# Wider rearranging DMAs for raw keys and values, key copies by DMA, and first queries' lower halves on VectorE, in a planned attention stage

## The chip, the cores and the metric

The kernel runs on one core of a Trainium2 chip. The metric is the time on the device in microseconds: the median of several executions. One execution was also taken by the hardware profiler; all rows below are of that one. Engines are named as the profile has them: PE is TensorE (matmuls; PEld its weight loads), DVE is VectorE, ACT is ScalarE, POOL is GpSimd, SP is SyncE, which here only issues DMAs.

## The reference

A decoder of two layers over 512 tokens of width 1024. Layer 0 is a gated short convolution and a squared-ReLU MLP. Then one shared key and value side is projected; layer 1 is sparse attention over it (16 heads in 4 groups of 64 channels) and another MLP. What matters here, cut down:

```python
def compress_blocks(t, pe, w1, w2):                    # t: (B,S,G,dh), blocks of 32, stride 16
    chunks = t.reshape(B, S // 16, 16, G, dh)
    blocks = jnp.concatenate([chunks[:, :-1], chunks[:, 1:]], axis=2) + pe[None, None, :, None, :]
    flat = jnp.moveaxis(blocks, 2, 3).reshape(B, 31, G, 32 * dh)
    return jax.nn.silu(flat @ w1) @ w2

kv = (rms_norm(x, kv_norm) @ w_kv).reshape(B, S, 6, N_KV_GROUPS, HEAD_DIM)
k_raw, v_raw, k_sel, v_sel, k_win, v_win = ...          # the six parts
k_cmp = compress_blocks(k_raw, cmp_pe_k, phi_k_w1, phi_k_w2)
v_cmp = compress_blocks(v_raw, cmp_pe_v, phi_v_w1, phi_v_w2)
# per query block: softmax attention over k_cmp, over selected blocks (all 8 of them, top_n = 16 > 8),
# and over the window of 512; the three are weighted by gates and summed; then w_o, then the MLP
```

With 512 tokens there are 8 selection blocks, fewer than the 16 that may be selected, and the window covers all tokens, so two of the three branches are full causal attention with their own keys and values.

## The kernel before, in words

All matrix products are made from 16-bit floats with each operand split in a high and a low half (`hi` is the rounded value, `lo` the rest), so one product is three matmuls. Activations lie transposed, channels on the 128 partitions and 512 tokens along the row; a `new_split` gives a pair of tiles, [128, 8, 512] each, for the halves.

Weights stream from memory in pieces. SyncE issues the load of a piece into one of three buffers `wst`; ScalarE converts it to `whi`, VectorE subtracts to get `wlo`, and the buffer is free for the piece three further on. Pieces are loaded and converted in the order in which they are used.

From 500 to 800 us runs the attention stage. Its instructions are not issued as the code meets them: they are held (`Plan.hold`), and `Plan.issue` writes out one order for each engine by simulating them. It knows each task's cost (`Plan.cost`, from constants per engine and the number of elements), how long a result takes to reach another engine, and when a DMA lands (`Plan.land`: 2050 ns and bytes over 325 per ns). A task becomes ready when those it depends on end; an engine takes the ready task with the smallest key, that is, the earliest in the code. Which tasks depend on each other `Plan.touch` finds from the box (partitions, first to last element of the row) that each operand spans. The order is fixed at build time; at run time each engine works in order and waits only for what its operands really need.

In that stage, `keys(br)`, `values(br)`, `queries(g)`, `gates`, `raw(which)` and `phi(which)` are background work, cut in units that a list of names, costs and due times (`AGENDA`) spreads between the attention items. The items (`Full`: a group, a block of 128 queries, a branch) compute scores (`st0`), exponentials, transposes, and products with values; `Cmp` items do the compressed branch. `keys(0)` and `queries(0)` come first; no item can begin without them.

- `keys(br)`: the product with the weights gives two PSUM banks `po`; each is scaled to `t` and holds two groups, 64 channels each on partitions 0–63 and 64–127. The score matmuls use all 128 rows: the query tile holds the query's high half on one set of 64 partitions and its low half on the other, and so the keys must stand on both. `KD[r, br, 0, g]` and `KD[r, br, 1, g]` are the high and low half on the group's own partitions `r`, `KD[o, ...]` the same on the other 64, `o`. Before, ScalarE and VectorE compute both copies.
- `queries(g)`: `q[r, h]` on ScalarE is the high half, `q[o, h]` on GpSimd the low half on the other partitions.
- `raw(which)` makes the keys (0) or values (1) that `phi(which)` compresses. Tokens are reordered so that the 16 places in a chunk come first (`r`, 16) and the 32 chunks follow (`b`, 32); `hl` holds the halves. `phi` multiplies for each of 16 pairs of places, so partitions 0–63 must hold a row and 64–127 the same row 32 columns on. This shift across partitions is done by DMAs from SyncE, into `big` for the keys and into the pair named `xs` (`xsh` and `xsl` in the profile) for the values.
- `phi` reads 31 columns from `at = 64 * (cc % 8) + cc // 8` on, for `cc` from 0 to 15.

Of the kernel before, what the change touches and what calls it, by code (L numbers as in the profile page):

```python
# [10 lines left out]
F32 = mybir.dt.float32  # L11
F16 = mybir.dt.float16
AF = mybir.ActivationFunctionType
OP = mybir.AluOpType
PSUM = bass.MemoryType.PSUM
DRAM = bass.MemoryType.DRAM


S, D, F, H, G, DH = 512, 1024, 4096, 16, 4, 64
# [26 lines left out]
class Plan:  # L46
# [83 lines left out]
    def cost(self, name, op, args, kwargs, out, ins):  # L130
        n = max(self.count(a) for a in out + ins)
        if name == "PE":
            n = self.count(out[0])
            if op == "transpose":
                return max(84.0, n / 128 * 109)
            if ins[0].dtype == F32:
                return 223.0 if n == 1 else n * 1.7
            return max(25.3, n * 0.4213)
        if "dma" in op:
            return 370.0  # L140
        if op == "memset":
            return 50 + 0.8 * n
        slope = self.SLOPE[name]
        if op == "tensor_copy" and ins[0].dtype == F16:
            slope *= 0.35
        return self.BASE[name] + slope * n + (189 if kwargs.get("accum_out") is not None else 0) + (
            20 if op == "tensor_tensor_reduce" else 0)

    def land(self, t, at):
# [74 lines left out]
class Held:  # L224
    ins = None
# [20 lines left out]
def body(ctx, tc, x, rel_bias, norm_mix, norm_mlp, mlp_w1, mlp_w2, a_w_in, a_conv_w, a_w_out,  # L246
# [4 lines left out]
    PE, ACT, DVE, POOL, SPQ = (plan.engine(e) for e in ("PE", "ACT", "DVE", "POOL", "SP"))  # L251
# [3 lines left out]
    work = ctx.enter_context(pool("work"))  # L255
# [206 lines left out]
    xt4 = wk[0].tile([128, 4, D], F32, name="xt")  # L462
    xt = [xt4[:, t] for t in range(4)]
# [28 lines left out]
    gain = {"mix0": 0, "mix1": 8, "mlp0": 16, "mlp1": 24, "kv": 32}  # L492

    def new_split(p, name, bufs=1):
        return tuple(p.tile([128, 8, S], F16, name=name + e, bufs=bufs) for e in "hl")

    def split_gain(dst, c, src, gname):

        g = vec[:, gain[gname] + c:gain[gname] + c + 1]
        hi = ACT.activation(dst[0][:, c], src, AF.Copy, scale=g)  # L500
        DVE.scalar_tensor_tensor(dst[1][:, c], src, g, dst[0][:, c], op0=OP.mult, op1=OP.subtract)
        return hi
# [67 lines left out]
    def ftile(name, bufs=2, n=S):  # L570
        return wk[0].tile([128, n], F32, name=name, bufs=bufs)

    def split_to(hi, lo, src, scale=1.0):
        ACT.activation(hi, src, AF.Copy, scale=scale)
        if scale == 1.0:
            DVE.tensor_tensor(lo, src, hi, op=OP.subtract)
        else:
            DVE.scalar_tensor_tensor(lo, src, scale, hi, op0=OP.mult, op1=OP.subtract)


    xs = new_split(wk[0], "x0")

    def x_chunk(c):
# [16 lines left out]


    ys = new_split(wk[0], "y")
    for p in range(4):
        pc, pu, pb = [], [], []
# [41 lines left out]
        for dst in (pc, pu, pb):  # L646
# [7 lines left out]
            for m in range(2):  # L654
                ch = 2 * p + m
                if dst is pc:
                    if m == 0:
                        tmps = []
                    t = ftile("cv_t", 2)
                    DVE.scalar_tensor_tensor(t, pc[m], 1.0 / (SY * SY), rb2, op0=OP.mult, op1=OP.mult)  # L660
                    tmps.append(t)
                elif dst is pu:
# [6 lines left out]
                    o = ftile("cv_o", 2)  # L669
# [13 lines left out]
    xs = new_split(work, "xs")  # L683
# [114 lines left out]
    def first_half(hp, xs, ss):  # L798
        rh = tuple(hp.tile([128, 8, 7, 256], F16, name=n) for n in ("rh", "rl"))
        rb = mlp_up(xs, ss, rh, 0, None)  # L800
        mlp_down(rh, None)
        mlp_up(xs, ss, rh, 1, rb)
        return rh
# [18 lines left out]
    with pool("attn") as ap_:  # L822
# [8 lines left out]
        KD = ap.tile([128, 2, 2, G, S], F16, name="KD")  # L831
# [30 lines left out]
        def rows_after_first():  # L862
            nonlocal rbk, rbq, rtok
            r = ss.r
            pr = broadcast_rows(r)
            rbk = row_tile(pr, SK / (SW * SX))
            rbq = row_tile(pr, SQ / 8.0 / (SW * SX))
            rtok = ap.tile([128, 2, 4], F32, name="rtok")
            DVE.tensor_scalar(rtok[:, 0], r, SV / (SW * SX), None, op0=OP.mult)
            DVE.tensor_scalar(rtok[:, 1], r, 0.5 / (SW * SX), None, op0=OP.mult)  # L870

        def scaled(ps, rb):
            t = ftile("at_s", 3)
            DVE.tensor_tensor(t, ps, rb, op=OP.mult)
            return t
# [6 lines left out]
        def gated_pair(xs, mid=None):  # L882

            po = [abank(), abank()]
            for half in range(2):
                w = next_piece()
                cv = ahead_fine()
                for c in range(4):
                    if mid and (half, c) == (1, 1):
                        mid()  # L890
                    for m in range(2):
                        k = 4 * half + c
                        mm3(po[m], [u[:, c, m * 128:(m + 1) * 128] for u in w], [u[:, k] for u in xs],
                            k == 0, k == 7)
                        next(cv, None)
                        yield 0.65
                drain(cv)
            return po
# [6 lines left out]
        def keys(br):  # L905
            po = yield from gated_pair(xkv, ss.rstd if rbk is None else None)
            if rbk is None:
                rows_after_first()
            for m in range(2):
                t = scaled(po[m], rbk)  # L910
                for s in range(2):
                    g, r = 2 * m + s, slice(64 * s, 64 * s + 64)
                    o = slice(64 - 64 * s, 128 - 64 * s)
                    ACT.activation(KD[r, br, 0, g], t[r], AF.Copy)
                    ACT.activation(KD[o, br, 0, g], t[r], AF.Copy)
                    DVE.tensor_tensor(KD[r, br, 1, g], t[r], KD[r, br, 0, g], op=OP.subtract)
                    DVE.tensor_tensor(KD[o, br, 1, g], t[r], KD[r, br, 0, g], op=OP.subtract)
                yield
            if br == 0:
                for c in range(8):  # L920
                    split_gain(xq, c, X[:, c], "mix1")
# [42 lines left out]
        def queries(g):  # L964
            po = yield from gated_pair(xq)
            q = ap.tile([128, 4, S], F16, name="Q", bufs=4)
            for m in range(2):
                t = scaled(po[m], rbq)
                for s in range(2):
                    h, r = 2 * m + s, slice(64 * s, 64 * s + 64)  # L970
                    o = slice(64 - 64 * s, 128 - 64 * s)
                    ACT.activation(q[r, h], t[r], AF.Copy)
                    POOL.tensor_tensor(q[o, h], t[r], q[r, h], op=OP.subtract)
                yield
            Qs[g] = q


        def raw(which):
            po = yield from gated_pair(xkv)
            if which == 0:  # L980
                both = ap.tile([128, 2, 8, S], F16, name="big", bufs=1)
                kr = [both[:, hl] for hl in range(2)]
            else:
                kr = new_split(work, "xs")
            for u in kr:
                DVE.memset(u[:, 4], 0.0)
                DVE.memset(u[64:128, 0:4, S - 1:S], 0.0)
            for half in range(2):
                at = slice(half, S, 64)
                split_to(kr[0][:, 4, at], kr[1][:, 4, at], pet[:, which, 8 * half:8 * half + 8], SK)  # L990
            both = ap.tile([128, 4, S], F16, name="kr_hl", bufs=1)
            for m in range(2):
                t = ftile("at_s", 3)
                by_stride = lambda a: a.rearrange("p (b r) -> p r b", r=16)
                DVE.tensor_tensor(t.rearrange("p (r b) -> p r b", r=16), by_stride(po[m]), by_stride(rbk),
                                  op=OP.mult)
                hl = both[:, 2 * m:2 * m + 2]
                split_to(hl[:, 0], hl[:, 1], t)
                for s in range(2):
                    g, r = 2 * m + s, slice(64 * s, 64 * s + 64)  # L1000
                    for k, u in enumerate(kr):
                        SPQ.dma_start(u[0:64, g, :], hl[r, k])
                        SPQ.dma_start(u[64:128, g, 0:S - 32], hl[r, k, 32:S])
                        SPQ.dma_start(u[64:128, g, S - 32:S - 1], hl[r, k, 1:32])
                yield
            KRs[which] = kr

# [376 lines left out]
        for i in range(len(items) + 6):  # L1384
# [8 lines left out]
            while credit > 0.0:  # L1393
                u = next(bg, "end")
# [15 lines left out]
    xs = xm  # L1410
# [3 lines left out]
    with pool("hidden_b") as hp:  # L1414
        wk[0] = hp
        rh = first_half(hp, xs, ss)
        xt = [work.tile([128, 2, D], F32, name=n) for n in ("xsh", "xsl")]
        xt = [xt[t // 2][:, t % 2] for t in range(4)]
        fng = [work.tile([128, S], F32, name="rb", bufs=3) for _ in range(2)]
        for half in range(2):  # L1420
            POOL.dma_start(fng[half], bass.AP(tensor=final_norm.tensor, offset=final_norm.offset + half * S,
                                                   ap=[[0, 128], [1, S]]))
# [137 lines left out]
```

## Time and profile before

| | |
|---|---|
| median of 3 runs | 1129.56 us (1128.71 to 1130.78) |
| profiled execution, own time | 1129.92 us |
| its span | 1128.2 us |
| mean granted TensorE clock | 0.993 of full speed |
| TensorE busy | 1095.0 us (97%) |
| VectorE busy | 875.1 us (78%) |
| ScalarE busy | 572.2 us (51%) |
| GpSimd busy | 56.2 us (5%) |

The span runs from the first to the last instruction of the profiled execution; its own time is a little longer. Busy times of engines overlap. A row of instructions reads: start and length in us (or a count with least, median and greatest length in ns), the engine, the line of the kernel, the operation, what it writes `<-` what it reads, the shapes, and in brackets how long the engine was idle before it and what ended that. Everything in the planned stage carries line 206, where the plan issues it, so rows there are told apart by their tiles. `SPq` is SyncE issuing DMAs: the length of such a row is the issue, not the transfer.

### The profile page before, as it was taken

The numbers are of one execution on the slowest core, as the hardware profiler recorded it, in microseconds if no ns is written. First come the engines' busy times: TensorE is split into PE (matmuls) and PEld (weight loads), VectorE is DVE, ScalarE is ACT, GpSimd is POOL, SyncE is SP. The second block draws the span as 40 slices with busy tenths as digits, with TensorE's granted clock in tenths as the row PEclk, the third lists the DMA queues.
The fourth block names the chain that finished last, engine by engine and source line by source line (L and its number), as shares of the span: only waits on it lengthen the run. The fifth ranks groups of instructions, "written<-read, shape, count | busy, mean of one in ns | idle before, by whom it ended". The sixth has DMA issues, their size and how long they took to land.

```text
span 1128.2 us, 20034 instructions
## 1 busy us (share of the span) xinstructions
PE 1095.0 (97%) x7959; PEld 695.6 (62%) x7959; DVE 875.1 (78%) x1642; ACT 572.2 (51%) x920; POOL 56.2 (5%) x71
## 2 busy tenths in 40 slices
PE   8999999999999999999999799899999999999996
PEld 4444444447884448876666676675444788444895
DVE  4755457987988768969688689997998798865776
ACT  3532244554334435547577679765754434442352
POOL 0000000000000000002010022212000000000010
PEclk9999999999999999999999899999999999999999
DMA  6433334533343332322324351012553333330221
GB/s 209 124 105 94 112 94 150 165 115 110 102 123 116 96 91 77 93 75 84 114 76 114 98 156 55 27 33 76 165 165 100 113 113 113 112 94 1 92 78 75
DMA packets 150050, 115.76 MB, mean 103 GB/s; under 512 B 9028, under 2 KB 146980, under 8 KB 149956
## 3 DMA queue, kind: packets, MB, share of 16 engines
q1 hardware_dynamic: 147120, 108.94, 32.3%
q10 hardware_dynamic: 2548, 4.93, 1.3%
q8 instruction: 62, 1.02, 0.4%
q0 software_dynamic: 288, 0.61, 0.2%
q14 instruction: 32, 0.26, 0.1%
HBM read 110.22 MB, written 2.14 MB: 100 GB/s over the span
## 4 chain that ended last, share of the span: by engine, by line
PE 83%; DVE 9%; ACT 2%; DMA 2%; issue 2%; SPq 1%; POOL 1%; DVEq 0%; ACTq 0%; POOLq 0%
PE c L240 23%; PE b L240 21%; PE a L240 20%; PE a L206 7%; PE d L240 4%; PE c L206 3%; DVE at_s L206 3%; PE e L240 2%; PE b L206 2%; DVE at_pl L206 2%; PE d L206 1%; SPq L206 1%; DVE wlo L206 1%; DVE o_t L206 1%; DMA xt<-x_dram 1%
## 5 line engine op out<-in xcount | busy, mean ns | idle before, releaser
L240 PEld LDWEIGHTS <-whi 128*128 128x128 f16 x3328 | 325.6, 98 | 200.9 <-issue 2.7
L240 ACT ACTIVATE whi<-wst 128x1024 f16<-128x1024 f32 (+2 forms) x162 | 209.2, 1297 | 279.1 <-PE b L240 96.4
L240 DVE SCALAR_TENSOR_TENSOR wlo<-wst,whi 128x1024 f16<-128x1024 f32 (+2 forms) x162 | 245.8, 1522 | 54.6 <-ACT whi L240 54.4
L240 PEld LDWEIGHTS <-wlo 128*128 128x128 f16 x1664 | 162.8, 98 | 101.5 <-issue 0.6
L240 DVE TENSOR_TENSOR wst<-wst 128x256 f32<-128x256 f32 x256 | 94.9, 418 | 21.4 <-DMA wst<-mlp_w_dram 20.2
L240 DVE TENSOR_TENSOR rl<-ml_z,rh 128x1792 f16<-128x1792 f32 x32 | 64.7, 2023 | 44.4 <-ACT rh L240 44.4
L240 ACT ACTIVATE rh<-ml_z 128x1792 f16<-128x1792 f32 x32 | 54.3, 1697 | 66.5 <-DVE ml_z L240 66.5
L206 ACT ACTIVATE at_p<-at_s,at_m 128x128 f32<-128x128 f32 (+3 forms) x128 | 70.9, 554 | 24.0 <-DVE at_m L206 22.6
L206 PEld LDWEIGHTS <-whi 128*128 128x128 f16 x512 | 48.0, 98 | 41.5 <-issue 4.2
L240 PE MATMUL c<-xsh,whi 128*128 128x512 f16 x192 | 72.8, 379 | 0.0
L240 PE MATMUL c<-xsl,whi 128*128 128x512 f16 x192 | 72.8, 379 | 0.0
L240 PE MATMUL c<-xsh,wlo 128*128 128x512 f16 x192 | 72.8, 379 | 0.0
L240 PE MATMUL b<-xsl,whi 128*128 128x512 f16 x192 | 72.8, 379 | 0.0
L240 PE MATMUL b<-xsh,wlo 128*128 128x512 f16 x192 | 72.8, 379 | 0.0
L240 PE MATMUL b<-xsh,whi 128*128 128x512 f16 x192 | 72.7, 379 | 0.0
L240 PE MATMUL c<-rh,whi 128*128 128x256 f16 x256 | 69.8, 273 | 0.0
L240 PE MATMUL c<-rh,wlo 128*128 128x256 f16 x256 | 69.8, 273 | 0.0
L240 PE MATMUL c<-rl,whi 128*128 128x256 f16 x256 | 69.8, 273 | 0.0
L240 PE MATMUL a<-rh,whi 128*128 128x256 f16 x256 | 69.1, 273 | 0.0
L240 PE MATMUL a<-rh,wlo 128*128 128x256 f16 x256 | 69.1, 273 | 0.0
L240 PE MATMUL a<-rl,whi 128*128 128x256 f16 x256 | 67.8, 273 | 0.0
L206 DVE SCALAR_TENSOR_TENSOR at_pl<-c,at_ph 128x512 f16<-128x512 f32 (+2 forms) x96 | 59.2, 618 | 9.5 <-ACT at_ph L206 9.3
(275 smaller groups left out, 2311.4 us busy)
## 6 DMA issues: line engine op xcount, KB each, us to landing
wst<-mlp_w_dram SPq DMA_DIRECT2D x256, 256.0 KB, 3.4
wst<-a_w_in_dram SPq DMA_DIRECT2D x18, 512.0 KB, 3.6
wst<-w_kv_dram SPq DMA_DIRECT2D x12, 512.0 KB, 3.7
T<-ext_d ACTq DMA_DIRECT2D x4, 1056.0 KB, 6.9
wst<-a_w_out_dram SPq DMA_DIRECT2D x8, 512.0 KB, 3.6
wst<-b_w_qg_dram SPq DMA_DIRECT2D x8, 512.0 KB, 3.8
wst<-b_w_o_dram SPq DMA_DIRECT2D x8, 512.0 KB, 3.6
wst<-a_w_in_dram SPq DMA_DIRECT2D x8, 384.0 KB, 5.9
```

The source lines that it names most:

```text
L206: getattr(self.engines[t["e"]], t["op"])(*t["args"], **t["kw"])
L240: return real(*args, **kwargs)
```

## The change

It has five parts.

1. `raw`: the tile for both halves is one, and each DMA moves both halves of a group to one set of partitions. The columns from 480 on are no longer filled: the third, short DMA goes, the long ones are cut to 480 columns, and the memset of the last column goes. 8 DMAs per call instead of 24.
2. `keys`: the copy on the other partitions is made by one DMA per group, from the copy just computed, instead of by a ScalarE and a VectorE instruction. 4 DMAs per call.
3. `queries`: for g = 0 the low halves are computed by VectorE, for the others by GpSimd as before.
4. The plan's costs: a DMA whose source is on the chip costs 640 instead of 370; instructions over at most 64 partitions and more than 256 elements cost 110 more; `scalar_tensor_tensor` on VectorE with a one-element operand 60 more; `tensor_tensor` over rows of 16 in reordered steps has 1.75 times the slope.
5. `new_split` gives the two halves of one tile, [128, 2, 8, 512], instead of two tiles; the names that share its memory follow (`xs`).

```diff
         if "dma" in op:
-            return 370.0
+            return 370.0 if ins[0].space == DRAM else 640.0
...
-        slope = self.SLOPE[name]
+        slope, base = self.SLOPE[name], self.BASE[name]
         if op == "tensor_copy" and ins[0].dtype == F16:
             slope *= 0.35
-        return self.BASE[name] + slope * n + (189 if kwargs.get("accum_out") is not None else 0) + (
+        if out[0].ap[0][1] <= 64 and n > 256:
+            base += 110
+        elif name == "DVE" and op == "scalar_tensor_tensor" and any(self.count(a) == 1 for a in ins):
+            base += 60
+        if op == "tensor_tensor" and ins and list(ins[0].ap)[-1][0] == 16:
+            slope *= 1.75
+        return base + slope * n + (189 if kwargs.get("accum_out") is not None else 0) + (
...
     def new_split(p, name, bufs=1):
-        return tuple(p.tile([128, 8, S], F16, name=name + e, bufs=bufs) for e in "hl")
+        t = p.tile([128, 2, 8, S], F16, name=name, bufs=bufs)
+        return t[:, 0], t[:, 1]
...
                     ACT.activation(KD[r, br, 0, g], t[r], AF.Copy)
-                    ACT.activation(KD[o, br, 0, g], t[r], AF.Copy)
                     DVE.tensor_tensor(KD[r, br, 1, g], t[r], KD[r, br, 0, g], op=OP.subtract)
-                    DVE.tensor_tensor(KD[o, br, 1, g], t[r], KD[r, br, 0, g], op=OP.subtract)
+                    SPQ.dma_start(KD[o, br, :, g], KD[r, br, :, g])
...
-                    POOL.tensor_tensor(q[o, h], t[r], q[r, h], op=OP.subtract)
+                    (POOL if g else DVE).tensor_tensor(q[o, h], t[r], q[r, h], op=OP.subtract)
...
-            if which == 0:
-                both = ap.tile([128, 2, 8, S], F16, name="big", bufs=1)
-                kr = [both[:, hl] for hl in range(2)]
-            else:
-                kr = new_split(work, "xs")
-            for u in kr:
-                DVE.memset(u[:, 4], 0.0)
-                DVE.memset(u[64:128, 0:4, S - 1:S], 0.0)
+            both = (ap.tile if which == 0 else work.tile)([128, 2, 8, S], F16, name="xs" if which else "big", bufs=1)
+            kr = [both[:, hl] for hl in range(2)]
+            DVE.memset(both[:, :, 4], 0.0)
...
-            both = ap.tile([128, 4, S], F16, name="kr_hl", bufs=1)
+            whole = ap.tile([128, 4, S], F16, name="kr_hl", bufs=1)
...
-                    for k, u in enumerate(kr):
-                        SPQ.dma_start(u[0:64, g, :], hl[r, k])
-                        SPQ.dma_start(u[64:128, g, 0:S - 32], hl[r, k, 32:S])
-                        SPQ.dma_start(u[64:128, g, S - 32:S - 1], hl[r, k, 1:32])
+                    SPQ.dma_start(both[0:64, :, g, 0:S - 32], hl[r, :, 0:S - 32])
+                    SPQ.dma_start(both[64:128, :, g, 0:S - 32], hl[r, :, 32:S])
...
-        xt = [work.tile([128, 2, D], F32, name=n) for n in ("xsh", "xsl")]
-        xt = [xt[t // 2][:, t % 2] for t in range(4)]
+        xt4 = work.tile([128, 4, D], F32, name="xs")
+        xt = [xt4[:, t] for t in range(4)]
```

More of the change, by code (lines that the diff above doesn't have):

```diff
@@ L996, in raw @@
                                   op=OP.mult)
-                hl = both[:, 2 * m:2 * m + 2]
+                hl = whole[:, 2 * m:2 * m + 2]
                 split_to(hl[:, 0], hl[:, 1], t)
```

## The prediction

> **What bounds the kernel now.** I read the page's summary first, then TensorE's stretches in the attention part, then the waits and the SyncE queue there.
>
> ```profile
> span 1128.2 us, 20034 instructions
> PE 1095.0 (97%) x7959; PEld 695.6 (62%) x7959; DVE 875.1 (78%) x1642; ACT 572.2 (51%) x920; POOL 56.2 (5%) x71
> ```
>
> The stretches (us from the span's start, length, busy time of each engine, granted clock), first the whole attention part, then four pieces of it with what follows them:
>
> ```profile
> core 0: us, PE busy (x) PEld busy (x) DVE busy (x) ACT busy (x) POOL busy (x), PEclk, DMA share, GB/s
> 500.00:800.00 300.00, 280.83 (x2836) 192.60 (x2834) 253.74 (x683) 216.60 (x546) 45.28 (x50) 0.98 0.29 87
> 508.00:528.00 20.00, 17.47 (x117) 10.59 (x116) 18.88 (x32) 14.66 (x27) 6.19 (x4) 1.00 0.26 80
> 560.00:564.00 4.00, 2.71 (x16) 1.39 (x14) 3.79 (x9) 3.95 (x11) 0.00 (x0) 1.00 0.00 0
> 615.00:617.40 2.40, 0.37 (x4) 0.09 (x3) 2.03 (x10) 1.36 (x6) 0.61 (x1) 1.00 0.27 58
> 617.40:621.00 3.60, 3.60 (x31) 3.24 (x32) 1.49 (x3) 2.07 (x5) 0.00 (x0) 0.53 0.75 193
> 621.00:634.40 13.40, 13.40 (x206) 12.29 (x203) 12.67 (x35) 8.10 (x22) 1.47 (x2) 1.00 0.33 73
> 634.40:641.20 6.80, 0.17 (x3) 0.00 (x0) 0.37 (x2) 1.66 (x4) 0.00 (x0) 0.76 0.73 218
> 641.20:644.40 3.20, 3.15 (x25) 2.56 (x26) 2.18 (x7) 3.13 (x11) 0.00 (x0) 0.50 0.10 33
> ```
>
> TensorE is 97% busy over the span, but 300 − 280.83 = 19.2 us of its 33.2 us idle lie in the planned attention part. Four stretches hold 12.5 us of that: 2.5 in 508–528, 1.3 in 560–564, 2.0 in 615–617.4, 6.6 in 634.4–641.2. After the last two the granted clock is about 0.5, the 1.2 GHz level, for 3.6 and 3.2 us. In the longest, VectorE and ScalarE do almost nothing either (0.37 and 1.66 us), so its whole length is on the path. Who waited for whom there (us in total, times, longest):
>
> ```profile
> PE a L206 <- DMA big<-kr_hl: 2.0, 1, 2.0
> ```
> ```profile
> ACT whi L206 <- DMA wst<-b_w_qg_dram: 7.8, 1, 7.8
> ...
> PE c L206 <- ACT at_p L206: 6.7, 1, 6.7
> ```
> ```profile
> PE b L206 <- DVE xql L206: 1.4, 1, 1.4
> PE a L206 <- ACT GT L206: 1.3, 1, 1.3
> PE b L206 <- POOL Q L206: 1.1, 3, 0.8
> ```
>
> And SyncE's queue, with the conversions that its weight loads feed or wait for:
>
> ```profile
> 596.54 19.73 SPq L206 DMA_DIRECT2D big<-kr_hl  x24
> ...
> 617.82 3.66 SPq L206 DMA_DIRECT2D xsh<-kr_hl  x6
> ...
> 632.08 2.97 SPq L206 DMA_DIRECT2D xsl<-kr_hl  x3
> 635.14 0.53 SPq L206 DMA_DIRECT2D wst<-b_w_qg_dram  x1
> ```
> ```profile
> 639.54 1.06 ACT L206 ACTIVATE whi<-wst 128x1024 f16<-128x1024 f32 x1 [7.83 <-DMA wst<-b_w_qg_dram]
> ```
> ```profile
> 625.65 1.29 DVE L206 SCALAR_TENSOR_TENSOR wlo<-wst,whi 128x512 f16<-128x512 f32 x2
> ```
>
> The 6.7 us is a weight load in the wrong place. SyncE issues the 48 rearranging copies of raw(0) and raw(1) almost without a pause from 596.5 to 635.1, and the second load of q2's weights stands behind them all. It is issued at 635.14. ScalarE, which works in order, stopped at 631.7 (639.54 − 7.83) to convert it; the exponentials behind it (at_p) come late, and TensorE with them. The 2.0 us is phi(0), waiting for raw(0)'s last copy.
>
> **The change part by part.**
>
> ```profile
> L206 SPq DMA_DIRECT2D big<-kr_hl x24: 462/595/1762, 596.5 to 615.5; - x24
> ...
> L206 DVE TENSOR_TENSOR kr_hl<-at_s,kr_hl x4: 681/690/692, 596.5 to 621.5; 128x512 f16<-128x512 f32 x4
> ...
> DMA to landing us min/median/max: 1.8/2.7/7.8
> ```
> ```profile
> big<-kr_hl SPq DMA_DIRECT2D x8, 64.0 KB, 3.7
> ...
> big<-kr_hl SPq DMA_DIRECT2D x8, 3.9 KB, 2.0
> ```
>
> *Wider copies of the raw keys and values.* Each raw() goes from 24 issues to 8: high and low halves travel in one DMA, and the columns past 480, which phi never reads (its last is 449 + 30), are dropped with their tiny third DMA and the memset. The old ones held SyncE 19.73 us in raw(0), 0.82 each, and 17.2 in raw(1) (617.82 to 635.05). The new form (64 partitions, two runs of 960 B) has no row. Bounds: 0.60 each if the issue is paid per instruction, for which the narrow spread around the median speaks (595 ns for copies of 64.0 and of 3.9 KB together); 1.19 if twice the runs cost twice. I take 0.64, the median and the small gap between two, so 5.1 us a raw. The Trainium skill, Perfetto Trace Analysis, § What "DMA-bound" means, says that an issuing track solid with DMA slices shows descriptor generation, and that large descriptors are what matter there. The runs do not grow here, so by that page the merged copies would cost the upper end, 9.5 us a raw, and the forecast would be an estimated 0.5 us later.
>
> What this gives. The second q2 load needs SyncE free and a buffer; that buffer is released by the low-half conversions that end at 626.94. raw(1)'s copies are then done: the second four are ready at 622.2 (621.5 + 0.69) and take 2.6 to 4.8 us. So the load goes out at about 627 instead of 635.14, lands 4.3 us later as it did (635.14 to about 639.5), at 631.3, against a demand at 631.7: the wait goes, with 0 to 1 us left over. Gain: 6.6 idle, plus half of the 3.2 us at half clock, 1.6, less 0.5: **7.7 us**. For phi(0), whose last copy was issued at 615.5, eight copies are out some 10 us sooner, so its 2.0 us go, and with them up to 1.7 of the 3.6 us at half clock. But from 621 to 634.4 VectorE is busy 12.67 of 13.4 us, so what is won may be capped by the 2.1 us that VectorE itself idled in 617.4–621. Between 2.1 and 3.7: **3.0 us**.
>
> ```profile
> L206 ACT ACTIVATE KD<-at_s x16: 614/628/630, 509.4 to 560.7; 64x512 f16<-64x512 f32 x16
> L206 DVE TENSOR_TENSOR KD<-at_s,KD x16: 674/686/690, 510.5 to 561.9; 64x512 f16<-64x512 f32 x16
> ```
> ```profile
> 521.27 6.41 POOL L206 TENSOR_TENSOR Q<-at_s,Q 64x512 f16<-64x512 f32 x4 [517.65 <-ACT Q L206]
> ```
> ```profile
> 528.51 0.28 DVE L206 CUSTOM_DVE_ANT_0 at_s<-b,T 128x128 f32<-128x128 f32 x1
> ```
>
> *Second copy of the keys by DMA.* Per keys() four ScalarE copies (4 × 0.628 = 2.5 us) and four VectorE subtractions (4 × 0.686 = 2.7 us) go; four SyncE issues come (2.4 us at the median above, 4.8 doubled). In the first call this frees VectorE, busy 18.88 of 20 us there, so xql is no longer late (1.4 us, counted two paragraphs on). In the second it takes 2.5 us off ScalarE ahead of GT: that wait of 1.3 us goes, unless the planner puts something else there. **1.0 us** of 0 to 1.3.
>
> The new cost is latency. The planner compares bounding boxes (L122), and one copy's box spans both halves, so it makes the next group's writes wait for the last group's copy. In rows, a group is 0.63 + 0.69 + 2.7 landing + 0.2 of hops = 4.2 us, and four from 509.4 are ready at 526.2, the first scores a us later. That would be hidden: attention's first step on VectorE starts at 528.51 now, held by GpSimd's 6.41 us for q0's four lower halves.
>
> *First queries' lower halves on VectorE.* Four subtractions like the row above at 0.69 instead of 6.41 us on GpSimd; they take back on VectorE the 2.7 us that the keys gave. The three waits of 1.1 us go. So attention starts about 1.3 us earlier, at 527.2, and up to 2.5 us of idle in 508–528 goes: **1.9 us**.
>
> *The rest.* One tile instead of two for each hi/lo pair moves no work. The planner's costs (640 for a copy within SBUF, +110, +60, ×1.75) move none either, but the whole order from 500 to 800 is made anew: 0 taken, ±3 us kept for the range.
>
> **Sum.** 7.7 + 3.0 + 1.0 + 1.9 = 13.6 us. The profiled execution took 1129.92 us (its span 1128.2 and 1.7 around it), 0.4 over the median of 1129.56: 1129.9 − 13.6 = **1116.3 us**. What is late next is VectorE against TensorE after 650 us; both reach that point earlier, so it takes nothing back.
>
> **The rivals.**
>
> *The q2 load is late all the same.* Its buffer is freed by VectorE, nearly full there. If those conversions end 4 us later against ScalarE's demand, a 4 us stop remains and, with the clock, costs 5: 1121. For it: only 0.4 us of slack by my sum. Against it: the planner knows that load and its buffer. Chance 0.2.
>
> *The copies really wait for each other*, since their boxes overlap. A pair then takes 1.2 + 2.7 us and a raw four pairs, 15.6, nearly as now: both big gains vanish, 1129.9 − 1.9 = 1128.
>
> ```profile
> 183.86 2.29 SPq L240 DMA_DIRECT2D wst<-mlp_w_dram  x4
> ```
> ```profile
> wst<-mlp_w_dram SPq DMA_DIRECT2D x256, 256.0 KB, 3.4
> ```
>
> Against it: these loads come in pairs that write interleaved runs of one tile (L374), and four are issued in 2.29 us, less than the landing of one. Chance 0.06.
>
> *Slower: the keys come late.* With the planner's chain, and copies landing at the 7.8 us maximum instead of 2.7, a group is 9.3 us, the first keys are ready at 546.6 and attention starts 20 us after the 527.2 above. All of it is paid if TensorE's other work is used up meanwhile: 1116.3 + 20 = 1136. It decides from a landing of about 6.1 us on. For it: SyncE's stragglers of 1.76 us, and weight loads in the same queue. Against it: the median. Chance 0.06.
>
> *More is won*: better costs also remove most of the other 6.7 us of idle in the attention part, 1110. Chance 0.06.
>
> **How the numbers follow.** The forecast has 0.62, the likeliest, with its own range 1112 to 1120 from the ±3 and the bounds above. Adding the late load and most of the larger gain gives 1110 to 1125 and leaves out under 2 in 10. Within 0.2% of no change (2.3 us, about what a measurement here can tell) lies the rival of waiting copies: 0.06. Slower is the late keys, with 0.02 for a new order that turned bad elsewhere: 0.08. Faster: 0.86.
>
> **What the changed profile would show.** Right: 16 copies of kr_hl with a median near 0.6 us; the second b_w_qg load within a microsecond of a low-half conversion's end; no wait of ScalarE on it over 1 us; granted clock 1.0 through 610–650; no TensorE wait on GT or on GpSimd's Q; attention's first at_s by 527.5. Wrong: copies of 1.2 us, or spaced by their landing; ScalarE stopped on another weight load; keys later than 528; TensorE idle over 10 us between 500 and 680.

## Result and the profile after

The changed kernel takes 1116.8 us (median of 4 runs, 1115.1 to 1117.3) where the kernel before takes 1129.4 in runs beside it: a ratio of 0.9884 [0.9867, 0.9902]. The profiled execution took 1116.31 us, its span 1114.4, at a mean clock of 0.998. All rows below are each of one execution. Rows of the planned stage carry line 212 in the kernel after, and the line of the layers' other rows is 246 instead of 240; in the experiments these numbers shift with the length of the plan's code (206 to 212, 240 to 246).

The head of the page after:

```profile
span 1114.4 us, 19969 instructions
PE 1091.7 (98%) x7959; PEld 693.9 (62%) x7959; DVE 868.7 (78%) x1632; ACT 565.8 (51%) x912; POOL 50.5 (5%) x67
```

The stretches after, with the columns of before: the attention part cut off at the same distance from the end (328.2 us), and the places of the four large idle stretches of before.

```profile
500.00:786.20 286.20, 278.31 (x2842) 191.56 (x2840) 248.96 (x674) 210.93 (x538) 39.61 (x46) 1.00 0.33 94
508.00:528.00 20.00, 20.00 (x149) 13.99 (x148) 17.64 (x31) 11.90 (x24) 0.00 (x0) 1.00 0.45 116
556.00:564.00 8.00, 8.00 (x72) 4.78 (x71) 6.82 (x20) 5.74 (x13) 0.00 (x0) 1.00 0.50 148
605.00:625.00 20.00, 20.00 (x283) 17.38 (x282) 17.95 (x51) 16.05 (x44) 2.21 (x3) 1.00 0.50 128
620.00:640.00 20.00, 19.46 (x196) 12.92 (x194) 17.91 (x52) 15.96 (x44) 0.73 (x1) 1.00 0.55 150
```

The attention part is 13.8 us shorter. TensorE's idle time in it fell from 19.2 to 7.9 us (286.20 − 278.31), which is 11.3; its busy time fell by 2.5 (280.83 − 278.31). That fits the matmuls that had run at the 1.2 GHz level for 3.6 and 3.2 us: the clock is 1.00 in all these stretches. What TensorE still waits for from 490 to 800 us:

```profile
PE a L212 <- DVE phi_t L212: 1.3, 1, 1.3
PE c L212 <- DVE at_pl L212: 1.2, 2, 0.7
...
PE d L246 <- DVE ssacc L212: 0.7, 1, 0.7
...
PE a L212 <- ACT GT L212: 0.3, 1, 0.3
```

No line is above 1.3 us, and the waits on at_p, on big's DMA, on xql and on GpSimd's Q are gone. SyncE's queue, then ScalarE's conversion, at the place of the old stop:

```profile
611.62 4.18 SPq L212 DMA_DIRECT2D xs<-kr_hl  x6
619.00 0.38 SPq L212 DMA_DIRECT2D wst<-b_w_qg_dram  x1
619.43 1.24 SPq L212 DMA_DIRECT2D xs<-kr_hl  x2
```
```profile
623.47 1.06 ACT L212 ACTIVATE whi<-wst 128x1024 f16<-128x1024 f32 x1
```

The second load of q2's weights goes out at 619.00, right after the low-half conversion that frees its buffer (617.68 and 1.29 long), and before the last two copies. ScalarE converts it with no bracket behind the row: it did not wait.

To see where the time came from in every kernel, I cut the span at four events, by the first or last start in the rows of three groups. Of before and then of after:

```profile
L206 PE MATMUL e<-whi,kr_hl x16: 192/193/193, 674.4 to 675.9; 128*128 128x64 f16 x16
...
L206 ACT ACTIVATE kr_hl<-at_s x4: 629/630/630, 595.9 to 620.7; 128x512 f16<-128x512 f32 x4
```
```profile
L206 PE MATMUL b<-KD,Q x256: 217/326/634, 523.4 to 772.1; 128*128 128x128 f16 x32, 128*128 128x256 f16 x32, 128*128 128x384 f16 x32, 128*128 128x512 f16 x32
```
```profile
L212 PE MATMUL e<-whi,kr_hl x16: 192/193/193, 658.7 to 660.3; 128*128 128x64 f16 x16
L212 SPq DMA_DIRECT2D big<-kr_hl x8: 590/614/1366, 593.5 to 600.5; - x8
L212 SPq DMA_DIRECT2D xs<-kr_hl x8: 590/594/610, 611.6 to 620.1; - x8
...
L212 ACT ACTIVATE kr_hl<-at_s x4: 616/629/632, 591.1 to 613.0; 128x512 f16<-128x512 f32 x4
...
DMA to landing us min/median/max: 2.3/2.5/5.4
```
```profile
L212 PE MATMUL b<-KD,Q x256: 216/300/380, 519.4 to 756.4; 128*128 128x128 f16 x33, 128*128 128x384 f16 x32, 128*128 128x512 f16 x32, 128*128 128x256 f16 x31
L212 ACT ACTIVATE KD<-at_s x8: 613/626/630, 509.3 to 566.1; 64x512 f16<-64x512 f32 x8
```

The sections: from the first key half (`KD<-at_s`) to raw(0)'s first split (`kr_hl<-at_s`) is "keys and queries"; from there to phi(1)'s output product (`e<-whi,kr_hl`) is "raw"; from there to the last score (`b<-KD,Q`) is "rest"; the last, to the end of the span, is "tail".

| us, one execution each | first key half at | keys and queries | raw | rest | tail | span |
|---|---|---|---|---|---|---|
| before | 509.4 | 86.5 | 78.5 | 97.7 | 356.1 | 1128.2 |
| after | 509.3 | 81.8 | 67.6 | 97.7 | 358.0 | 1114.4 |

So 4.7 us were won ahead of raw, 10.9 in raw, nothing in the rest, and 1.9 were given back in the tail.

### The profile page after: what moved, and what is told of

Its sections match the earlier page's. It is cut to its first block, busy times and chain, and to the rows that moved or that the text cites. A ratio compares the mean times of both kernels' runs of the same rounds, so it can differ in the third digit from the quotient of the medians.

```text
span 1114.4 us, 19969 instructions
## 1 busy us (share of the span) xinstructions
PE 1091.7 (98%) x7959; PEld 693.9 (62%) x7959; DVE 868.7 (78%) x1632; ACT 565.8 (51%) x912; POOL 50.5 (5%) x67
## 4 chain that ended last, share of the span: by engine, by line
PE 86%; DVE 7%; ACT 3%; DMA 2%; issue 2%; POOL 0%; SPq 0%; DVEq 0%; POOLq 0%; ACTq 0%
PE c L246 22%; PE b L246 20%; PE a L246 19%; PE a L212 11%; PE d L246 4%; PE b L212 3%; PE c L212 3%; PE e L246 2%; PE d L212 2%; DVE at_s L212 1%; DVE at_pl L212 1%; DVE wlo L246 1%; DMA wst<-b_w_qg_dram 1%; DVE o_t L212 1%; DMA wst<-a_w_in_dram 0%
## 5 line engine op out<-in xcount | busy, mean ns | idle before, releaser
L246 PE MATMUL b<-xs,whi 128*128 128x512 f16 x384 | 114.3, 379 | 0.0
L246 PE MATMUL c<-xs,whi 128*128 128x512 f16 x384 | 114.2, 379 | 0.0
L246 PE MATMUL a<-xs,whi 128*128 128x512 f16 x256 | 76.1, 379 | 0.0
L246 PE MATMUL c<-xs,wlo 128*128 128x512 f16 x192 | 72.8, 379 | 0.0
L246 PE MATMUL b<-xs,wlo 128*128 128x512 f16 x192 | 72.8, 379 | 0.0
L212 DVE CUSTOM_DVE_ANT_0 at_s<-b,T 128x128 f32<-128x128 f32 (+3 forms) x128 | 59.1, 483 | 5.3 <-PE b L212 5.0
```

Source lines behind the costliest of these rows:

```text
L212: getattr(self.engines[t["e"]], t["op"])(*t["args"], **t["kw"])
L246: return real(*args, **kwargs)
```

## The experiments

The theory at first was the prediction's: SyncE's 48 issues are what delays the load and phi(0), so fewer issues are the gain. Its rivals: the order that the planner makes with other costs does it, or only the place of the load in the queue matters. Median times are set against runs of the kernel before on the same chip.

**Only the new raw() and the one-tile pair**, the rest as before (parts 1 and 5 alone):

```diff
-                    for k, u in enumerate(kr):
-                        SPQ.dma_start(u[0:64, g, :], hl[r, k])
-                        ...
+                    SPQ.dma_start(both[0:64, :, g, 0:S - 32], hl[r, :, 0:S - 32])
+                    SPQ.dma_start(both[64:128, :, g, 0:S - 32], hl[r, :, 32:S])
```

> The kernel before with the new raw() alone (8 wide copies per call; with it the one-tile pairs, which it needs), old costs, keys and queries as before. Theory (SyncE's issues hold up the second q2 load and phi(0)'s last copy): 10.7 us of the gain are here, so 1118 to 1121 us, ScalarE's wait on the q2 load under 1.5 us and TensorE's wait on the copies gone. Rival (the gain comes from the new order of the stage, not from the copies): 1126 us or more.

1118.62 us, ratio 0.9901 [0.9888, 0.9914]. The load goes out 12 us earlier than before (635.14), and ScalarE's conversion waits 0.56 us:

```profile
623.06 0.37 SPq L206 DMA_DIRECT2D wst<-b_w_qg_dram  x1
```
```profile
627.69 1.06 ACT L206 ACTIVATE whi<-wst 128x1024 f16<-128x1024 f32 x1 [0.56 <-DMA wst<-b_w_qg_dram]
```

The raw section takes 67.2 us, as in after; keys and queries 86.4, as in before. The wider copies alone bring the large gain, in the way that the prediction described.

**Everything but the new raw()**: 24 narrow copies per call, with the new costs.

```diff
-                    SPQ.dma_start(both[0:64, :, g, 0:S - 32], hl[r, :, 0:S - 32])
-                    SPQ.dma_start(both[64:128, :, g, 0:S - 32], hl[r, :, 32:S])
+                    for k, u in enumerate(kr):
+                        SPQ.dma_start(u[0:64, g, :], hl[r, k])
+                        ...
```

> The changed kernel with the old raw() (24 narrow copies per call), everything else new. Theory: only the parts at the keys, the first queries and the costs are left, 3 to 5 us, so 1124 to 1127 us, with a ScalarE wait of several us on a q2 load. Rival (the new order is what counts): 1117 to 1120 us with no such wait.

1116.64 us, ratio 0.9892 [0.9875, 0.9908]. The theory missed: with all 48 copies back, the time is that of the changed kernel. The load is still behind all 48 (the last goes out at 628.0), and ScalarE hardly waits:

```profile
628.72 0.53 SPq L212 DMA_DIRECT2D wst<-b_w_qg_dram  x1
```
```profile
632.89 1.06 ACT L212 ACTIVATE whi<-wst 128x1024 f16<-128x1024 f32 x1 [0.99 <-DMA wst<-b_w_qg_dram]
```

**High and low halves copied apart**, 16 copies per raw(), the rest as after:

```diff
-                    SPQ.dma_start(both[0:64, :, g, 0:S - 32], hl[r, :, 0:S - 32])
-                    SPQ.dma_start(both[64:128, :, g, 0:S - 32], hl[r, :, 32:S])
+                    for k in range(2):
+                        SPQ.dma_start(both[0:64, k, g, 0:S - 32], hl[r, k, 0:S - 32])
+                        SPQ.dma_start(both[64:128, k, g, 0:S - 32], hl[r, k, 32:S])
```

> The changed kernel with the high and low halves copied apart: 16 copies of 480 columns per raw() instead of 8, same bytes, no box that spans both halves. Theory by issue count: 8 more issues of 0.64 us per call; the load of q2 goes out up to 2.6 us later, and 0 to 3 us of the gain are lost: 1117 to 1120 us. Rival (the planner's chain of boxes holds phi back and costs more than the issues): faster than the changed kernel, 1114 to 1116 us.

1118.17 us, ratio 0.9899 [0.9886, 0.9912]: inside what the theory said, but its interval overlaps that of after, so the two are not told apart. ScalarE's wait from 600 to 640 us:

```profile
ACT whi L212 <- DMA wst<-b_w_qg_dram: 2.2, 1, 2.2
```

That is more than with 24 copies per call above, so the number of issues alone doesn't order the waits; the table behind the last of the price runs shows why.

**Loads from memory first on SyncE**, the kernel before otherwise:

```diff
+        if name == "SP" and ins and ins[0].space == DRAM:
+            t["key"] -= 1000000
```

> The kernel before, with one line in the plan: loads from memory on SyncE go ahead of its other tasks as soon as they are ready. All 48 narrow copies stay. Theory (the 6.7 us stop is a load queued in the wrong place): that stop and its half-clock time go, about 8 us, the 2.0 us of phi(0) stays or grows by the time of a load: 1121 to 1124 us. Rival (the copies themselves are late for what follows, wherever the load stands): 1127 to 1130 us, with the stop moved to phi(1) or phi(0).

1128.01 us, ratio 0.9982 [0.9973, 0.9991]. A miss: the load passed only one copy, and ScalarE stopped for 6.21 us instead of 7.83. Why it passed no more is not shown: the simulation's times are not on record, but a planner that counts the copies too short would see the load become ready only near their end.

```profile
631.94 0.53 SPq L208 DMA_DIRECT2D wst<-b_w_qg_dram  x1
632.51 0.53 SPq L208 DMA_DIRECT2D xsl<-kr_hl  x1
```
```profile
635.94 1.06 ACT L208 ACTIVATE whi<-wst 128x1024 f16<-128x1024 f32 x1 [6.21 <-DMA wst<-b_w_qg_dram]
```

The second and the fourth run together point to ScalarE's written order. The new theory: the planner priced a copy within SBUF at 0.37 us where the change says 0.64, so over a raw() of 24 copies its clock for SyncE was at least 24 × 0.27 = 6.5 us early (the 24 copies took 17.2 to 19.7 us), twice that over two. It therefore believed in an early load and put ScalarE's conversion too early in ScalarE's order for the load that came. At run time the in-order engine stood still there. Fewer copies or a right price would each mend it.

**Only the price**, the kernel before otherwise; 48 copies stay:

```diff
-            return 370.0
+            return 370.0 if ins[0].space == DRAM else 640.0
```

> The kernel before with one line of the plan changed: a copy within SBUF is priced 640 instead of 370. All 48 narrow copies stay. New theory (the stop comes from the plan's price: it put ScalarE's conversion 48 x 0.27 = 13 us of copies too early): the second q2 load still goes out behind the copies, near 628 to 635, but its conversion stands later in ScalarE's order, the 6.7 us stop goes: 1118 to 1122 us. First theory (the copies must be fewer): 1126 us or more, stop of several us.

1120.22 us, ratio 0.9917 [0.9900, 0.9933]: 9.4 us from one line that changes no instruction. SyncE's queue, then ScalarE:

```profile
629.62 1.87 SPq L206 DMA_DIRECT2D xsl<-kr_hl  x3
631.59 0.54 SPq L206 DMA_DIRECT2D wst<-b_w_qg_dram  x1
```
```profile
635.33 0.71 ACT L206 ACTIVATE at_p<-at_s,at_m 128x512 f32<-128x512 f32 x1
635.94 0.19 ACT L206 ACTIVATION_READ_ACCUMULATOR at_p<-at_s,at_m 128x1 f32 x1
636.04 1.04 ACT L206 ACTIVATE whi<-wst 128x1024 f16<-128x1024 f32 x1
```

The load goes out at 631.59, behind all 48 copies, as before. ScalarE does exponentials and steps of phi up to 636.04 and only then converts, without a wait. Between the conversion of the piece before and this one its order has 30 instructions, where the kernel before has 7. The raw section is 69.0 us instead of 78.5.

**The second run without the price** (48 copies, all else new, price 370 again):

```diff
-            return 370.0 if ins[0].space == DRAM else 640.0
+            return 370.0
```

> The changed kernel with the old raw() (24 narrow copies) and the old price of 370 for a copy, the other new costs kept: the one that came out at 1116.6 us, less one line. New theory: the stop comes back, 4 to 8 us and its half clock: 1122 to 1127 us. Rival (something else in the new order, not the price, hid the copies): 1116 to 1118 us.

1125.87 us, ratio 0.9968 [0.9957, 0.9979]: the stop is back, at about the same issue time as with the price (627.89 against 628.72), and the clock with it:

```profile
632.52 1.06 ACT L212 ACTIVATE whi<-wst 128x1024 f16<-128x1024 f32 x1 [7.98 <-DMA wst<-b_w_qg_dram]
```
```profile
600.00:640.00 40.00, 32.50 (x391) 25.76 (x390) 28.56 (x94) 27.44 (x85) 2.26 (x4) 0.91 0.47 125
```

**The changed kernel without the price** (the same line, 16 wide copies):

> The changed kernel with the old price of 370 for a copy, one line undone; 16 wide copies stay. Theory (the stop is the number of copies times the error of the price: now 8 x 0.24 = 2 us a call instead of 24 x 0.27 = 6.5): no long stop, at most 2 us on a q2 load, 1116.5 to 1119 us. Rival (the price matters by itself): 1120 us or more.

1116.48 us, ratio 0.9886 [0.9871, 0.9901]. With 16 copies the price error does no harm. These runs make a table (median us, ratio to before with its interval; "new" is with parts 2 and 3 and the other costs of part 4; one-tile pairs go with either new part):

| | price 370 | price 640 |
|---|---|---|
| 48 copies, else old | 1129.4 (before) | 1120.22, 0.9917 [0.9900, 0.9933] |
| 48 copies, else new | 1125.87, 0.9968 [0.9957, 0.9979] | 1116.64, 0.9892 [0.9875, 0.9908] |
| 16 copies, else old | 1118.62, 0.9901 [0.9888, 0.9914] | not run |
| 16 copies, else new | 1116.48, 0.9886 [0.9871, 0.9901] | 1116.8, 0.9884 [0.9867, 0.9902] (after) |

Only 48 copies at the price of 370 have the stop of 6 to 8 us, with and without the rest. Either remedy is worth some 9 to 11 us; beside the other, in the lower rows with the new rest, neither adds anything that can be measured. The one-tile pairs were not run by themselves.

The two remedies work differently, as ScalarE's order and the load's time in the traces show. The instructions are those between the conversion of the piece before and this one; ScalarE comes to it at its start less its wait:

| | load goes out at | ScalarE's instructions in between | ScalarE comes to it at | and waits |
|---|---|---|---|---|
| before | 635.14 | 7 | 631.71 | 7.83 |
| loads first | 631.94 | 7 | 629.73 | 6.21 |
| 48 copies, price 370, else new | 627.89 | 7 | 624.54 | 7.98 |
| 48 copies, price 640, else old | 631.59 | 30 | 636.04 | none |
| 48 copies, price 640, else new | 628.72 | 30 | 631.90 | 0.99 |
| 32 copies, price 640, else new | 623.61 | 9 | 626.40 | 2.22 |
| 16 copies, price 370, else old | 623.06 | 7 | 627.13 | 0.56 |
| 16 copies, price 370, else new | 619.24 | 7 | 623.57 | 0.18 |
| after | 619.00 | 7 | 623.47 | none |

In the runs with a wait the conversion begins 4.0 to 5.0 us after the load's issue. The price moves the consumer back by 23 instructions and leaves the load behind all 48 copies. Fewer copies leave the consumer in its place and bring the load forward; that is what the changed kernel does, and the price of 640 moves nothing there. With 32 copies the load is earlier than with 48, but the consumer stands at 9 instead of 30, hence the longer wait.

**Keys' second copy on ScalarE and VectorE again**, the rest as after:

```diff
                     ACT.activation(KD[r, br, 0, g], t[r], AF.Copy)
+                    ACT.activation(KD[o, br, 0, g], t[r], AF.Copy)
                     DVE.tensor_tensor(KD[r, br, 1, g], t[r], KD[r, br, 0, g], op=OP.subtract)
-                    SPQ.dma_start(KD[o, br, :, g], KD[r, br, :, g])
+                    DVE.tensor_tensor(KD[o, br, 1, g], t[r], KD[r, br, 0, g], op=OP.subtract)
```

> The changed kernel with the second copy of the keys made by ScalarE and VectorE again. Theory of the prediction: xq late by 1 to 1.4 us in 508 to 528, the gate wait of 1.3 us back: 1118 to 1120 us. Rival (the new order hides these instructions): 1116 to 1117.5 us. Other rival (the DMA's latency held attention back to 528.2, so without it attention starts earlier): 1114 to 1116 us.

1116.77 us, ratio 0.9887 [0.9869, 0.9906]: no difference. A wait of TensorE for xq is back, but attention's first step comes at 524.61 instead of 528.17:

```profile
PE b L212 <- DVE xq L212: 1.5, 1, 1.5
```
```profile
524.61 0.28 DVE L212 CUSTOM_DVE_ANT_0 at_s<-b,T 128x128 f32<-128x128 f32 x1
```

TensorE's wait for GT is 0.3 us here too, so it is not the key DMAs that shorten it.

**KD laid out by groups**, the rest as after, so that the box of a copy no longer covers the next group's columns and the planner sees no false dependence:

```diff
-        KD = ap.tile([128, 2, 2, G, S], F16, name="KD")
+        KD = ap.tile([128, 2, G, 2, S], F16, name="KD")
...
-                    SPQ.dma_start(KD[o, br, :, g], KD[r, br, :, g])
+                    SPQ.dma_start(KD[o, br, g], KD[r, br, g])
```

> The changed kernel with KD laid out group by group, so that a group's two halves are one contiguous box (2 KB runs): the plan sees no false dependence between groups. Theory (the plan's boxes hold the keys): the four key copies are issued by 516 instead of 524.88, attention's first at_s comes at 523 to 526 instead of 528.2; time 1114 to 1117 us. Rival (the copies wait on the chip, not in the plan): still 4 us apart, no change in time.

1115.19 us, ratio 0.9872 [0.9854, 0.9891]: the lowest median of all, but not told apart from after by its interval. SyncE's key copies of the first call in after, and then in this kernel with its first step of attention:

```profile
510.67 0.65 SPq L212 DMA_DIRECT2D KD<-KD  x1
...
515.08 0.62 SPq L212 DMA_DIRECT2D KD<-KD  x1
...
520.84 0.60 SPq L212 DMA_DIRECT2D KD<-KD  x1
...
524.88 0.60 SPq L212 DMA_DIRECT2D KD<-KD  x1
```
```profile
510.73 2.58 SPq L212 DMA_DIRECT2D KD<-KD  x4
```
```profile
521.99 0.28 DVE L212 CUSTOM_DVE_ANT_0 at_s<-b,T 128x128 f32<-128x128 f32 x1
```

Four copies in 2.58 us instead of 14.8 (510.67 to 525.48): the chain of group after group was written by the planner, the chip doesn't ask for it. They follow VectorE's four subtractions, which take 2.84 us there. Attention starts 6.2 us earlier (521.99 against 528.17), and the keys-and-queries section stays at 82.0 us: TensorE had other work there.

**The same with the other costs undone** (+110, +60, ×1.75 taken out, 640 kept):

```diff
-        if out[0].ap[0][1] <= 64 and n > 256:
-            base += 110
-        elif ...
-            base += 60
-        if op == "tensor_tensor" and ins and list(ins[0].ap)[-1][0] == 16:
-            slope *= 1.75
```

> The kernel with KD group by group (1115.2 us), of the new costs only the price 640 kept (+110, +60 and x1.75 undone). Theory (those three put the end of the attention stage in a worse order, TensorE then waits 0.7 us on ssacc and from its last score to the end it takes 357.5 to 358 us instead of 356 to 356.8): 1114.0 to 1115.0 us, no wait on ssacc. Rival (they help elsewhere in the stage): 1116 us or more.

1118.90 us, ratio 0.9906 [0.9891, 0.9921]: a miss, these costs help. Without them keys and queries take 84.2 us instead of 82.0 and the rest of the stage 100.8 instead of 97.8; only the tail is shorter, 356.8 against 357.8. The two intervals meet at 0.9891, so the size, 3.7 us, is loose.

**q0's lower halves on GpSimd again**, the rest as after:

```diff
-                    (POOL if g else DVE).tensor_tensor(q[o, h], t[r], q[r, h], op=OP.subtract)
+                    POOL.tensor_tensor(q[o, h], t[r], q[r, h], op=OP.subtract)
```

> The changed kernel with q0's lower halves on GpSimd again. Theory of the prediction (GpSimd's 6.4 us hold the start of attention; this part is worth up to 1.3 us with the waits of 1.1): 1117 to 1119 us. Rival (the key copies, ready about 527, hold the start to 528.2 anyway, so the part is worth nothing here): 1116 to 1117.2 us, attention's first at_s still at 528 to 529.

1116.74 us, ratio 0.9889 [0.9874, 0.9904]; attention's first step at 528.09, as in after. Part 3 is worth nothing beside the others. That the key copies' place in the plan sets that step is argued from the layout by groups, where it comes at 521.99.

**KD and raw's tile both laid out by groups**:

```diff
+            both = both.rearrange("p a b s -> p (a b s)").rearrange("p (g k s) -> p k g s", k=2, s=S)
```

> KD and the tile of raw() both laid out group by group, all new costs: the plan sees no false dependence at any copy. Theory (the boxes also hold back phi in the plan): 1113 to 1115 us. Rival (raw's copies have slack in the plan, only the keys mattered): as with KD alone, 1115 to 1115.8 us.

1116.18 us, ratio 0.9882 [0.9865, 0.9898]: no further gain.

The sections of all runs, as above:

| us | first key half at | keys and queries | raw | rest | tail | span |
|---|---|---|---|---|---|---|
| new raw() alone | 508.5 | 86.4 | 67.2 | 97.7 | 356.8 | 1116.6 |
| price alone | 508.1 | 86.4 | 69.0 | 97.8 | 356.7 | 1118.0 |
| loads first | 509.5 | 86.4 | 76.4 | 97.9 | 356.7 | 1126.9 |
| old raw(), price 370 | 509.3 | 82.7 | 76.7 | 97.8 | 357.6 | 1124.1 |
| old raw(), price 640 | 509.5 | 82.6 | 67.5 | 98.9 | 357.4 | 1115.9 |
| 16 copies per raw() | 511.5 | 81.8 | 68.7 | 98.0 | 357.6 | 1117.6 |
| after, price 370 | 509.5 | 81.8 | 67.7 | 97.7 | 358.0 | 1114.7 |
| keys on the engines | 509.2 | 83.2 | 67.4 | 97.6 | 357.6 | 1115.0 |
| q0 on GpSimd | 509.4 | 81.7 | 67.0 | 98.0 | 358.0 | 1114.1 |
| KD by groups | 509.3 | 82.0 | 66.5 | 97.8 | 357.8 | 1113.4 |
| the same, old other costs | 508.9 | 84.2 | 67.1 | 100.8 | 356.8 | 1117.8 |
| KD and raw by groups | 508.8 | 82.0 | 67.5 | 98.9 | 357.6 | 1114.8 |

The raw section has two values, 76 to 79 us with the stop and 66 to 69 without. The section of keys and queries has 86.4 or 86.5 wherever parts 2 to 4 are old (the price aside) and 81.7 to 82.7 where they are new, also with part 3 undone; undoing part 2 makes it 83.2, undoing the other costs 84.2.

## Why the prediction was right, and where it was not

**The place of the gain.** The two places were right: the stop in 634–641 and phi(0)'s wait are gone, and the clock is 1.00. The two terms together, 7.7 + 3.0 = 10.7 us, stand against 10.9 in the raw section. Their shares can be estimated: with the price alone phi(0) still waits, and the stop is gone.

```profile
PE a L206 <- DMA big<-kr_hl: 1.6, 1, 1.6
```

There the raw section is 69.0 us, against 67.2 with the new raw() alone, which has no such wait. So the stop took about 78.5 − 69.0 = 9.5 us and phi(0)'s wait about 1.8: the first term was too small by some 2 us and the second too large by some 1.

**The mechanism of the large term** was right for this kernel: with 16 copies the load goes out earlier (619.00), ScalarE's conversion stands where it stood in its order, and the stop is gone, at either price.

**The step that failed** is "the planner's costs … move none either … 0 taken". The price line alone brings 9.4 us; beside the 16 copies it adds nothing, so the sum did not suffer from it. The other three costs do move time beside the rest: 2.2 us in the section of keys and queries, and some of the tail (both below). The diagnosis was half of the truth, too. The text called the stop a load in the wrong place, behind 48 issues. With the price alone the load stands in that place still (631.59) and nobody waits, because ScalarE now comes to its conversion at 636.04 where it had come at 631.7. So the stop was the distance between a late load and an early consumer, and either end could be moved. The row of before that hinted at the second was there: `big<-kr_hl x24` took 19.73 us, and the planner counted 24 × 0.37 = 8.9.

**The price of a wide copy.** 0.64 us each and 5.1 a raw() were nearly right: medians are 614 and 594 ns; in raw(1) six go out in 4.18 us and two in 1.24, 5.4 together, and in raw(0), where one took 1366 ns, the issues take 5.9. The load out within a microsecond of a low-half conversion's end was right too (619.00), though 8 us earlier than the 627 of the text, 4.8 of them because raw came that much sooner. The prediction took its upper end, 1.19 us each, from reading the Trainium skill, Perfetto Trace Analysis, § What "DMA-bound" means, which says that large descriptors are what matter on a solid issuing track. This trace does not bear that reading out: twice the runs per copy, no longer than before, left the issue in a series at 594 to 614 ns, against 595.

**Keys and queries.** Forecast 1.0 + 1.9 = 2.9 us, measured 4.7. The 2.5 us of idle in 508–528 and the 1.3 in 560–564 went. The terms were put down to the wrong parts: undoing part 3 costs nothing, undoing part 2 costs 1.4 us of the section (83.2 against 81.8) and nothing of the time. Undoing the other costs gives 2.2 us back in the section, 84.2 against 82.0 (in the layout by groups). They had been counted at nothing here too. The sign "no TensorE wait on GT" failed by 0.3 us, and the wait is 0.3 with the keys on the engines too.

**The keys' latency.** The chain through the planner's boxes was real, and a little slower than said: issues 4.7 us apart ((524.88 − 510.67) / 3) instead of 4.2, and attention's first step at 528.17, 0.3 us sooner than before instead of 1.3, so the sign "by 527.5" failed. That it would be hidden was right, and more so than argued: a start 6.2 us earlier shortened the section by nothing.

**What is given back.** "Takes nothing back" held up to the last score (97.7 us in both) and failed after it: the tail is 1.9 us longer. In it TensorE is idle 1.7 us more, 0.7 of it the wait on ssacc shown above, and 0.5 a wait on X near the end, the second of these rows, that before lacks:

```profile
PE c L246 <- DVE X L246: 0.7, 1, 0.7
PE a L246 <- DVE X L246: 0.5, 1, 0.5
```

The tails go by the costs: 356.1 to 356.8 us with the old other costs, 357.4 to 358.0 with the new; the wait on ssacc is in all nine kernels with the new ones and in none with the old, and it goes when they are undone in the layout by groups. The wait on X is not theirs: the new raw() alone, with old costs, has it with 0.7. Which of +110, +60 and ×1.75 makes the tail longer, and which wins the time ahead of it, was not tried.

So the sum of 13.6 met 13.8 of the span (12.6 by the medians) because two misses cancel, which is luck: 1.8 too little at the keys and queries, 1.9 not counted in the tail. Of the rivals, the load is not late, the copies do not wait for each other (six in 4.18 us, less than the landing of two), and the keys were not late enough to reach TensorE. Nor is more won: 7.9 us of idle are left in the attention part, where the four stretches taken away would have left 6.7.

A small stop of the same kind is left, one of the prediction's signs of being wrong (ScalarE stopped on another weight load). ScalarE's rows around q3's load, with VectorE's and TensorE's that follow from them:

```profile
654.36 1.06 ACT L212 ACTIVATE whi<-wst 128x1024 f16<-128x1024 f32 x1 [1.31 <-DMA wst<-b_w_qg_dram]
...
655.32 0.71 ACT L212 ACTIVATE at_p<-at_s,at_m 128x512 f32<-128x512 f32 x1
...
656.27 0.36 ACT L212 ACTIVATE phi_t<-a,phi_b 128x124 f32<-128x124 f32 x1
...
657.10 0.35 DVE L212 SCALAR_TENSOR_TENSOR phi_t<-a,phi_b,phi_t 128x124 f32<-128x124 f32 x1
...
657.50 0.59 PE L212 MATMUL a<-xq,whi 128*128 128x512 f16 x2 [1.34 <-DVE phi_t L212]
```

ScalarE stood 1.31 us before the conversion, phi's steps come behind it in its order, and TensorE's largest remaining wait, 1.34 us on phi_t, ends after them. That the one makes the other is read from the order of the rows; no run took it away.

## What to carry to other kernels

Where a program writes the order of in-order engines from a table of costs, set the table against the trace before looking for work to remove: one price wrong by 0.27 us, times 48 instructions, was worth about as much as removing two thirds of them. When an engine stands before a late input, compare the input's time and the consumer's place in its engine's order, and count what stands in between in a run with the stop and in one without; moving the consumer moves no data. And two cures of one stop don't add: undo each by itself before crediting either.

## What the runs showed of the hardware

SyncE's issue of a copy within SBUF hardly depends on its bytes. In a series the median is 595 ns for the narrow copies of 3.9 and 64 KB, and 594 to 614 for the wide ones, which carry 120 KB (64 partitions, two runs of 960 B). In issues with a pause between them the runs per partition do show. The key copies with two runs, in after, against one run of twice the length, in the layout by groups:

```profile
L212 SPq DMA_DIRECT2D KD<-KD x8: 596/597/653, 510.7 to 567.4; - x8
```
```profile
L212 SPq DMA_DIRECT2D KD<-KD x8: 461/484/1011, 510.7 to 556.5; - x8
```

The least is 461 ns against 596. Landing didn't grow with the wider copies either: the median is 2.5 us, after 2.7 before, and the longest 5.4, after 7.8.
